# An attention layer's last border: earlier queries, query tiles kept in key buffers, and two output tiles started half

## The chip, the cores and the metric

The kernel runs on one core of a Trainium2 chip. The metric is the device time of one launch in microseconds, as the median of several runs; shorter is better. TensorE multiplies (PE in the profile, with its weight loads as PEld), VectorE (DVE), ScalarE (ACT) and GpSimd (POOL) work on tiles, and SyncE (SP) issues most of the transfers from memory.

## The reference, cut to what matters

Two layers of a diffusion backbone over 512 latent tokens and 256 context tokens, 1024 features wide. The change lies in layer 0, windowed attention with 16 query heads that share 4 key and value heads:

```
q, k, v = split(h @ w_qkv); q = rope(rms_norm(q)); k = rope(rms_norm(k))
for each block of 128 latent queries:
    scores = [q.k_context, q.k_window] / 8          (window: the block and its two neighbours)
    p = softmax([scores, sink]);  o = p[context].v_context + p[window].v_window
context queries: the same, over the 256 context keys alone
x = x + gate * (o_x @ w_o);  ctx = ctx + gate_c * (o_c @ w_o)
```

Then a SwiGLU layer, a retention layer and a second SwiGLU layer follow, which the change does not touch.

## The kernel before, in words

Features lie on the 128 partitions and tokens along the free axis, so a weight tile of 128 output features is a column of eight 128x128 blocks. To keep float32 accuracy on TensorE's faster format, each operand is split into a high and a low part (`split`, lines 162 to 165: ScalarE copies the high part, VectorE subtracts for the low one), and one product becomes three matmuls (`mm3`, lines 143 to 149).

Attention runs in four groups `g` of one key head and four query heads. Each group has six blocks `(s, b)`: four of latent queries (`s` = 0) and two of context queries (`s` = 1). I write a block as (g, i), where i is its place in the group's order. The loop is at lines 828 to 845, and `attend` does this for one block:

- `score` (line 678): per head, TensorE makes the scores in one of three PSUM banks `S`; VectorE evicts them with the mask and the running maximum (L704) into a row tile `pr`, of which there are nine; per pair of heads ScalarE takes exponentials (L101) and GpSimd divides by the sum (L717).
- `turn` (line 721): per key tile, TensorE transposes the four heads' probabilities (L726) into one of two PSUM banks `pT`, and ScalarE or VectorE, in turn, copies them out (L728).
- `output` (line 733): TensorE multiplies with the values (L740) into the one bank `pO`; VectorE copies the result to `o_raw` (L755), or, in the last group, splits it straight into `o_t`.

Between the blocks the loop places other work. `make_q(j)` (line 559) makes the query heads 2j and 2j+1: 24 matmuls 512 wide over the latent tokens, 24 matmuls 256 wide over the context tokens into the two PSUM banks `pj`, then `shape` (rope, split into `q` tiles) and `norms` (row factors; the scores use them at eviction). It is called after blocks 1 and 3 of groups 0 to 2, for the next group. `q` tiles come from a ring of nine: two per j for the latent tokens, one for the context. A group's key tiles `k` are two of a ring of eight, and are not read after the group's last latent block.

From block (2, 4) on, `PARTS_AT` says how many of the stored `o_raw` halves are split into `o_t` after each block (18 in all), so that the output projection has its operands. The stored tiles share a ring with the residual stream, so a split also frees the room into which `load_stream` loads the context and latent streams. In the last group (order: context block 0, latent 0, context 1, latent 1, 2, 3) `context_out(d, w)` makes context output tile d whole, 24 matmuls 256 wide over all eight feature blocks, for d = 2 after block 3, d = 3 and 0 after block 4, and d = 1 after block 5. Each needs its weights loaded (`w_raw`, a ring of two, on SP's queue) and split.

The loop as it stands:

```
    for g in range(NKV):
        final = g == NKV - 1
        for i, (s, b) in enumerate((latent + context, latent + context, mixed, late)[g]):
            copy = attend(g, s, b)
            if not final and i in (1, 3):
                for piece in make_q(2 * g + 2 + i // 3):
                    piece()
            if (g, i) >= SPLIT_AT:
                first = len(parts_o) == 18
                for _ in range(PARTS_AT[g, i]):
                    parts_o.pop(0)([copy])
                if first:
                    wo0 = wpos[0]
                    cres = load_stream(1)
            for d in {3: early[:1], 4: early[1:3], 5: early[3:]}.get(i, ()) if final else ():
                wpos[0] = wo0 + d
                wo_w[d] = next_w(ap, 0)
                context_out(d, wo_w[d])
```

After the loop the latent output projection follows, 24 matmuls 512 wide for each of eight tiles, a dense stretch for TensorE.

The order of instructions on each engine is settled by a scheduler at build time; every engine's queue then runs in that order, and an instruction that waits holds what is behind it.

Of the kernel before, what the change touches and what calls it, by code (L numbers as in the profile page):

```python
# [9 lines left out]
F32R = mybir.dt.float32r  # L10
# [4 lines left out]
P = 128  # L15
D = 1024
KT = D // P
SX = 512
SC = 256
HD = 64  # L20
NH = 16
NKV = 4
# [4 lines left out]
EPS = 1e-6  # L27
UNITS = (4, 5, 8, 6)
WO_ADA = [(0, d) for d in range(8)]
SPLIT_AT = (2, 4)  # L30
HALVES = (slice(0, 256), slice(256, 512))

C_ADAB = 0
# [16 lines left out]
def dit_kernel(ctx, tc, xT, cT, crow, small, consts, masks, tabs0, tabs1, jtab, adaQ, adaN, adaT, wst, out):  # L50
# [11 lines left out]
    def T(pool, cols, tag, bufs, dt=F32):  # L62
        return pool.tile([P, cols], dt, tag=tag, bufs=bufs, name=tag)

    def pj(n=512):
        return T(psJ, 512, "pj", 2)[:, :n]
# [51 lines left out]
    wpos, wsel, ring = [0], [0], []  # L118

    def w_raw(pool=None, bufs=2):  # L120
        raw = T(pool or rp, 1024, "wraw", bufs)
        nc.sync.dma_start(raw, wst[wpos[0]])
        wpos[0] += 1
        return raw

    def w_parts(pool, own=2):

        bufs = own
        if ring:
            pool, bufs = ring[wsel[0] % len(ring)], 2  # L130
        elif wsel[0] % (2 + own) < 2:
            pool, bufs = rp, 2
        wsel[0] += 1
        return T(pool, 1024, "whi", bufs, F32R), T(pool, 1024, "wlo", bufs, F32R)

    def next_w(pool, own=2, raw=None, behind=(), late=()):

        raw = raw or w_raw()
        w = w_parts(pool, own)
        after(split(raw, *w, behind), late)  # L140
        return w

    def mm3(o, w, x, first, last):

        whi, wlo = w
        xhi, xlo = x
        nc.tensor.matmul(o, whi, xhi, start=first, stop=False)  # L147
        nc.tensor.matmul(o, wlo, xhi, start=False, stop=False)  # L148
        return nc.tensor.matmul(o, whi, xlo, start=False, stop=last)  # L149

    def project(w, hs, o):
        for k in range(KT):
            mm3(o, (w[0][:, k * P:(k + 1) * P], w[1][:, k * P:(k + 1) * P]), hs[k], k == 0, k == KT - 1)
# [14 lines left out]
    def load_stream(s, engines=(nc.sync, nc.sync)):  # L168
        res = []
        if s == 0:  # L170
            for k in range(KT):
                t = T(rp, 512, "res", 12)
                eng = engines[k % 2] if k < 4 else nc.sync
                ins = eng.dma_start(t, xT[:, k, :])
                if eng is nc.scalar:
                    turn["lnexp"].append(ins)
                res.append(t)
        else:
            for k in range(0, KT, 2):
                t = T(rp, 512, "res", 12)  # L180
                nc.sync.dma_start(t.rearrange("p (a n) -> p a n", a=2), cT[:, k:k + 2, :])
                res += [t[:, 0:SC], t[:, SC:2 * SC]]
        return res

    def t_sq(n):
        return T(rp, 512, "sq", 2)[:, :n]
# [180 lines left out]
    akv = AK.enter_context(tc.tile_pool(name="akv", bufs=1, reuse_waits="tile"))  # L367
# [152 lines left out]
    ap = At.enter_context(tc.tile_pool(name="ap", bufs=1, reuse_waits="tile"))  # L520
# [36 lines left out]
    q, stats = {}, {}  # L557

    def make_q(j, raw=None):

        if raw is None:
            w = next_w(ap, 0)
            parts_of = lambda k: (w[0][:, k * P:(k + 1) * P], w[1][:, k * P:(k + 1) * P])
        else:

            rows = [[T(ap, 656, "pr", PRB, F32R)[:, :512] for _ in range(2)] for _ in range(2)]
            for i, (hi, lo) in enumerate(rows):
                split(raw[:, i * 512:(i + 1) * 512], hi, lo)  # L570
            parts_of = lambda k: [t[:, k % 4 * P:(k % 4 + 1) * P] for t in rows[k // 4]]
        qs = T(ap, 64, "qs", 4)[:, 0:36].rearrange("p (f n) -> p f n", f=3)
        sqs, o = [], [None, None]

        def part(s, k0, k1):
            if k0 == 0:
                o[s] = pj(NTOK[s])
            for k in range(k0, k1):
                mm3(o[s], parts_of(k), h[s][k], k == 0, k == KT - 1)

        def shape(s):
            n = NTOK[s]
            sq, qn = t_sq(n), t_hn(n)
            nc.scalar.activation(qn, o[s], AF.Identity, scale=qk_gain[:, 0:1])
            nc.scalar.activation(sq, o[s], AF.Square)
            sqs.append(sq)
            if s == 0:
                sw = t_y(s)
                nc.vector.stream_shuffle(sw, qn, swap16)
                nc.gpsimd.tensor_tensor(qn, qn, rope0[:, 0:512], op=mult)  # L590
                nc.vector.tensor_tensor(sw, sw, rope0[:, 512:1024], op=mult)
                nc.vector.tensor_tensor(qn, qn, sw, op=add)
            qa = T(ap, 512, "q", 9, F32R)
            if s == 0:
                qb = T(ap, 512, "q", 9, F32R)
            else:
                qa, qb = qa[:, 0:SC], qa[:, SC:2 * SC]
            nc.scalar.copy(qa[0:64, :], qn[0:64, :])
            nc.scalar.copy(qb[64:128, :], qn[64:128, :])
            nc.vector.tensor_tensor(qa[64:128, :], qn[0:64, :], qa[0:64, :], op=sub)  # L600
            nc.vector.tensor_tensor(qb[0:64, :], qn[64:128, :], qb[64:128, :], op=sub)
            q[2 * j, s] = qa
            q[2 * j + 1, s] = qb

        def norms():
            tot = pj(12)
            for s, sq in enumerate(sqs):
                for b in range(NTOK[s] // P):
                    c = 8 * s + 2 * b
                    nc.tensor.matmul(tot[:, c:c + 2], sq[:, b * P:(b + 1) * P], bd[:, 0:P:64], start=True, stop=True)  # L610
            y, u, z = qs[:, 0], qs[:, 1], qs[:, 2]
            neg_half_rstd(y, z, tot, HD)
            nc.vector.scalar_tensor_tensor(u, tot, HD * EPS, y, add, mult)
            ue = u.rearrange("p (b e) -> p e b", e=2)
            for e in range(2):
                hd = 2 * j + e
                nc.vector.tensor_scalar(ue[:, e], ue[:, e], nsink[:, hd:hd + 1], -4.0 / HD, op0=mult, op1=mult)
                stats[hd] = qs

        def first():  # L620
            part(0, 0, 5)

# [12 lines left out]
    with tc.manual_schedule(engines={mybir.EngineType.PE}):  # L635
# [10 lines left out]
        for e in range(2):  # L646
            k1, k2 = key_parts(e, kn[1], "kc", 4)
# [18 lines left out]
    o_t = [[None] * KT, [None] * KT]  # L666
# [143 lines left out]


    early = [2, 3, 0, 1]
    wo_w = {}

    def context_out(d, w):
        o = pj(SC)
        project(w, o_t[1], o)
        ins = gated_add(1, 0, 2, d, o, cres)
        add_square(1, int(d != early[0]), cres[d])
        return ins  # L820
# [1 line left out]
    latent, context = [(0, b) for b in range(4)], [(1, b) for b in range(2)]  # L822
    mixed = [latent[0], latent[1], context[0], latent[2], latent[3], context[1]]
    late = [context[0], latent[0], context[1], latent[1], latent[2], latent[3]]
    parts_o = [p for sb in ((0, 0, 0), (0, 1, 0), (1, 1, 0), (2, 1, 0), (0, 0, 1), (1, 0, 0), (1, 0, 1),
                            (2, 0, 0), (2, 0, 1)) for p in splits_o(*sb)]
    PARTS_AT = {(2, 4): 2, (2, 5): 3, (3, 0): 3, (3, 1): 2, (3, 2): 2, (3, 3): 2, (3, 4): 2, (3, 5): 2}
    for g in range(NKV):
        final = g == NKV - 1
        for i, (s, b) in enumerate((latent + context, latent + context, mixed, late)[g]):  # L830
            copy = attend(g, s, b)
            if not final and i in (1, 3):
                for piece in make_q(2 * g + 2 + i // 3):
                    piece()
            if (g, i) >= SPLIT_AT:
                first = len(parts_o) == 18
                for _ in range(PARTS_AT[g, i]):
                    parts_o.pop(0)([copy])
                if first:
                    wo0 = wpos[0]  # L840
                    cres = load_stream(1)
            for d in {3: early[:1], 4: early[1:3], 5: early[3:]}.get(i, ()) if final else ():
                wpos[0] = wo0 + d
                wo_w[d] = next_w(ap, 0)
                context_out(d, wo_w[d])
    assert not parts_o
    xr = load_stream(0)
# [10 lines left out]
    for d4 in range(0, KT, 4):  # L858
        wpos[0] = wo0 + max(d4, 2)
        w = [next_w(wo_p) if d > 1 else wo_w[d] for d in range(d4, d4 + 4)]  # L860
        if d4 == 0:
            cr = cond_rows(wo_p)
        for d in range(d4, d4 + 4):
            o = pj(SX)
# [304 lines left out]
    qa = R.enter_context(tc.tile_pool(name="qa", bufs=1, reuse_waits="tile"))  # L1169
# [168 lines left out]
    for hd in range(RH):  # L1338
# [172 lines left out]
        for i in range(2):  # L1511
            g, v = chunk(bg + i), chunk(bv + i)
# [70 lines left out]
        w = []  # L1583
# [335 lines left out]
```

## Time and profile before

| quantity | value |
|---|---|
| time, median of 3 runs (lowest to highest) | 1747.34 us (1747.12 to 1749.5) |
| span of the profiled execution, first to last instruction | 1744.4 us |
| its own time | not recorded apart; the median less the span is 2.9 us |
| TensorE / VectorE / ScalarE / GpSimd busy | 98% / 77% / 49% / 8% |
| norms of the last queries begin; value products of block (2, 4) end | 252.0 us; 270.1 us |

Times in the profile count from the first instruction. "Busy" of PE is modelled: matmuls are pipelined, so two neighbours overlap, and a PE that is busy may still be waiting in part. A column "PEclk" gives the granted clock, 1.00 being full speed. In rows of groups, the time behind "idle before" is what the engine waited before those instructions, with who ended the wait.

### The profile page before, as it was taken

To read this page: it belongs to the slowest core of one execution; us is meant where nothing else is said; L and a number is where in the kernel's file an instruction comes from. 1 tells how busy PE (TensorE), PEld (TensorE's weight loads), DVE (VectorE), ACT (ScalarE), POOL (GpSimd) and SP (SyncE) were. 2 spreads that over 40 slices of the span, in tenths; PEclk is the share of its full clock that TensorE was granted. 3 is DMA by queue.
4 is the path that set the end of the run, shared out by engine and by line. 5 is a ranking of instruction groups with operands and counts; after the bars stand their busy time and mean duration, and the time that the engine had idled before them with its cause. 6 is when DMAs were issued, how large, how long until landed. Compare 5 with 4: busy or idle time off the path is not lost.

```text
span 1744.4 us, 27605 instructions
## 1 busy us (share of the span) xinstructions
PE 1712.7 (98%) x10876; PEld 1527.8 (88%) x10876; DVE 1350.5 (77%) x2368; ACT 846.3 (49%) x1492; POOL 131.0 (8%) x270
## 2 busy tenths in 40 slices
PE   7999999999999999999999999999999999999999
PEld 5777777899999999999988888898898899999997
DVE  6697778788778788787889858758768798777774
ACT  5576667465433334342456534525525565445442
POOL 0035435000000000000000000000000000000000
PEclk9999999999999999999999999999999999999999
DMA  9501012533243534343423524423423224233322
GB/s 353 230 13 38 13 43 68 204 122 135 71 147 121 158 109 145 123 153 101 156 99 86 182 84 130 162 86 121 157 85 118 76 84 132 77 117 101 104 79 85
DMA packets 59602, 203.54 MB, mean 117 GB/s; under 512 B 6608, under 2 KB 6992, under 8 KB 59216
## 3 DMA queue, kind: packets, MB, share of 16 engines
q1 hardware_dynamic: 51984, 175.03, 30.9%
q0 software_dynamic: 7200, 26.22, 5.2%
q8 instruction: 85, 1.39, 0.3%
q10 hardware_dynamic: 288, 0.52, 0.1%
q14 instruction: 45, 0.37, 0.1%
HBM read 199.65 MB, written 2.10 MB: 116 GB/s over the span
## 4 chain that ended last, share of the span: by engine, by line
PE 80%; DVE 8%; DMA 5%; ACT 3%; issue 2%; POOL 1%; SPq 0%; ACTq 0%; POOLq 0%; DVEq 0%
PE Y L886 15%; PE Z L886 7%; PE pj L147 6%; PE pj L148 6%; PE pj L149 6%; PE Z L1268 6%; PE X L886 4%; PE Y L1257 3%; PE pj L1268 2%; PE pT L726 2%; PE X L1257 2%; DMA wraw<-in_wst_dram 2%; PE pO L740 2%; PE S L703 2%; DMA adan<-in_adaQ_dram 1%
## 5 line engine op out<-in xcount | busy, mean ns | idle before, releaser
L164 ACT CAST whi<-wraw 128x1024 fp32r<-128x1024 f32 x258 | 270.2, 1051 | 370.7 <-PE Z L149 88.5
L165 DVE TENSOR_TENSOR wlo<-wraw,whi 128x1024 fp32r<-128x1024 f32 x258 | 315.0, 1223 | 60.9 <-ACT whi L164 59.7
L886 PE MATMUL Y<-aq,whi 128*128 128x384 f32 x640 | 173.7, 335 | 0.5 <-ACT sq L1044 0.5
L256 DVE SCALAR_TENSOR_TENSOR res<-pj,mod,res 128x512 f32<-128x512 f32 (+1 forms) x112 | 81.5, 729 | 65.6 <-PE pj L149 65.0
L886 PEld LDWEIGHTS Y<-aq,whi 128*128 128x128 f32 x640 | 116.6, 188 | 1.7 <-ACT sq L1044 0.9
L273 DVE CUSTOM_DVE_ANT_0 y<-adaw,crow,small_sb 128x1024 bf16<-128x1024 f32 x64 | 81.9, 1280 | 36.0 <-DMA adaw<-in_adaT_dram 35.7
L886 PE MATMUL Y<-aq,wlo 128*128 128x384 f32 x320 | 107.0, 334 | 0.0
L101 ACT ACTIVATE pr<-pr,stat,qs 128x513 f32<-128x513 f32 (+2 forms) x96 | 74.4, 777 | 23.5 <-DVE stat L710 22.9
L1268 PE MATMUL Z<-whi,sA 128*128 128x512 f32 x256 | 81.0, 391 | 1.2 <-ACT gate L1454 1.2
L717 POOL TENSOR_SCALAR pr<-pr,stat 128x512 f32<-128x512 f32 (+2 forms) x96 | 70.2, 744 | 79.5 <-DVE stat L714 54.8
L147 PE MATMUL pj<-ax,whi 128*128 128x512 f32 x176 | 68.8, 391 | 0.1
L149 PE MATMUL pj<-ax,whi 128*128 128x512 f32 x176 | 68.7, 390 | 0.0
L148 PE MATMUL pj<-ax,wlo 128*128 128x512 f32 x176 | 68.5, 389 | 0.0
L147 PE MATMUL pj<-act,whi 128*128 128x512 f32 x168 | 66.0, 393 | 0.0
L148 PE MATMUL pj<-act,wlo 128*128 128x512 f32 x168 | 65.9, 392 | 0.0
L149 PE MATMUL pj<-act,whi 128*128 128x512 f32 x168 | 65.5, 390 | 0.0
L270 POOL DMA_DIRECT2D adaw<-in_adaT_dram x48 | 25.6, 533 | 514.9 <-DVE mod L273 413.6
L726 PE MATMUL pT<-const_sb,pr 128*128 128x128 f32 x352 | 57.4, 285 | 6.1 <-POOL pr L717 3.6
L886 PE MATMUL Y<-sA,whi 128*128 128x256 f32 x304 | 60.6, 282 | 0.2 <-ACT res L1721 0.2
L886 PEld LDWEIGHTS Y<-aq,wlo 128*128 128x128 f32 x320 | 60.1, 188 | 0.0
L726 PEld LDWEIGHTS pT<-const_sb,pr 128*128 128x128 f32 x352 | 39.1, 142 | 23.0 <-POOL pr L717 12.4
L1268 PEld LDWEIGHTS Z<-whi,sA 128*128 128x128 f32 x256 | 48.0, 188 | 11.7 <-ACT gate L1454 1.9
(576 smaller groups left out, 5150.3 us busy)
## 6 DMA issues: line engine op xcount, KB each, us to landing
wraw<-in_wst_dram SPq DMA_DIRECT2D x224, 512.0 KB, 3.7
adaw<-in_adaT_dram POOLq DMA_DIRECT2D x48, 512.0 KB, 3.9
wx<-in_wst_dram SPq DMA_DIRECT2D x30, 512.0 KB, 4.3
adan<-in_adaQ_dram SPq DMA_DIRECT2D x16, 512.0 KB, 8.5
adan<-in_adaN_dram SPq DMA_DIRECT2D x12, 512.0 KB, 7.8
adaw<-in_adaT_dram SPq DMA_DIRECT2D x8, 512.0 KB, 3.9
res<-in_xT_dram SPq DMA_DIRECT2D x14, 256.0 KB, 3.8
aq<-in_adaN_dram SPq DMA_DIRECT2D x12, 256.0 KB, 5.8
```

Source lines behind the costliest of these rows:

```text
L101: ins = nc.scalar.activation(*args, **kw)
L147: nc.tensor.matmul(o, whi, xhi, start=first, stop=False)
L148: nc.tensor.matmul(o, wlo, xhi, start=False, stop=False)
L149: return nc.tensor.matmul(o, whi, xlo, start=False, stop=last)
L164: after(nc.scalar.copy(hi, t), behind)
L165: return nc.vector.tensor_tensor(lo, t, hi, op=sub)
L256: return nc.vector.scalar_tensor_tensor(res[d], o, mods[l, s][:, part, d:d + 1], res[d], mult, add)
L273: res.append(nc.vector.tensor_tensor_reduce(junk, w, cr[:, s * 1024:(s + 1) * 1024], 1.0, sm_t[:, C_ADAB + l * 48 + j:C_ADAB + l * 48 + j ...
L726: nc.tensor.transpose(tp[:, a * P:(a + 1) * P], self.pr[(0, 2, 1, 3)[a]][:, ki * P:(ki + 1) * P], ident)
L886: nc.tensor.matmul(o, p, r, start=first and k + i == 0, stop=k == 3 and i == 2, skip_group_check=not first)
L1257: ins = nc.tensor.matmul(o[:, e * SC:(e + 1) * SC], p[:, ws], r, start=first and k + e + i == 0, stop=k == 3 and i == 2, skip_group_check= ...
L1268: ins = nc.tensor.matmul(os[t], p, r, start=first and k + i == 0, stop=k == 3 and i == 2, skip_group_check=by_k or not first)
```

## The change

- `make_q` for the last group's queries (j = 6 and 7) is called after blocks 0 and 2 of group 2, where it was called after 1 and 3. Groups 0 and 1 keep 1 and 3.
- For j = 5 and 7 the two latent query tiles come from the ring of key tiles `k` (room of groups 0 and 1, which are done), not from the ring `q`.
- The splits of stored outputs start after block (2, 3), two after each block, and in another order: the context halves of groups 0 and 1 come first.
- New: `context_begin(d, behind)` loads and splits the weights of context tile d and makes its first half, the 12 matmuls over feature blocks 0 to 3 (heads 0 to 7), into a `pj` bank that stays held. It is called for d = 2 after block (2, 4) and for d = 3 after block (2, 5). `context_out` then makes the other 12 where it made all 24. Both `pj` banks are held from there until those tiles are done.

```
-SPLIT_AT = (2, 4)
+SPLIT_AT = (2, 3)
...
-            qa = T(ap, 512, "q", 9, F32R)
+            room = (akv, 512, "k", 8, F32R) if s == 0 and j in (5, 7) else (ap, 512, "q", 9, F32R)
+            qa = T(*room)
             if s == 0:
-                qb = T(ap, 512, "q", 9, F32R)
+                qb = T(*room)
...
+    def context_part(o, w, k0, k1):
+        for k in range(k0, k1):
+            mm3(o, (w[0][:, k * P:(k + 1) * P], w[1][:, k * P:(k + 1) * P]), o_t[1][k], k == 0, k == KT - 1)
+
+    def context_begin(d, behind):
+        wpos[0] = wo0 + d
+        wo_w[d] = next_w(ap, 0, behind=behind)
+        begun[d] = pj(SC)
+        context_part(begun[d], wo_w[d], 0, 4)
+
     def context_out(d, w):
-        o = pj(SC)
-        project(w, o_t[1], o)
+        o = begun.pop(d, None)
+        if o is None:
+            o = pj(SC)
+            project(w, o_t[1], o)
+        else:
+            context_part(o, w, 4, KT)
...
-    parts_o = [p for sb in ((0, 0, 0), (0, 1, 0), (1, 1, 0), (2, 1, 0), (0, 0, 1), (1, 0, 0), (1, 0, 1),
+    parts_o = [p for sb in ((0, 1, 0), (1, 1, 0), (0, 0, 0), (2, 1, 0), (0, 0, 1), (1, 0, 0), (1, 0, 1),
                             (2, 0, 0), (2, 0, 1)) for p in splits_o(*sb)]
-    PARTS_AT = {(2, 4): 2, (2, 5): 3, (3, 0): 3, (3, 1): 2, (3, 2): 2, (3, 3): 2, (3, 4): 2, (3, 5): 2}
+    PARTS_AT = {(2, 3): 2, (2, 4): 2, (2, 5): 2, (3, 0): 2, (3, 1): 2, (3, 2): 2, (3, 3): 2, (3, 4): 2, (3, 5): 2}
+    BEGIN_AT = {(NKV - 2, 4): early[0], (NKV - 2, 5): early[1]}
...
-            if not final and i in (1, 3):
-                for piece in make_q(2 * g + 2 + i // 3):
+            if not final and i in ((0, 2) if g == NKV - 2 else (1, 3)):
+                for piece in make_q(2 * g + 2 + i // 2):
...
+            if (g, i) in BEGIN_AT:
+                context_begin(BEGIN_AT[g, i], [copy])
             for d in {3: early[:1], 4: early[1:3], 5: early[3:]}.get(i, ()) if final else ():
-                wpos[0] = wo0 + d
-                wo_w[d] = next_w(ap, 0)
+                if d not in wo_w:
+                    wpos[0] = wo0 + d
+                    wo_w[d] = next_w(ap, 0)
                 context_out(d, wo_w[d])
```

More of the change, by code (lines that the diff above doesn't have):

```diff
@@ L812, in dit_kernel @@
     early = [2, 3, 0, 1]
-    wo_w = {}
-    def context_out(d, w):
-        o = pj(SC)
-        project(w, o_t[1], o)
+    wo_w, begun = {}, {}
+    def context_part(o, w, k0, k1):
[6 more added lines that the diff above has]
+        context_part(begun[d], wo_w[d], 0, 4)
+    def context_out(d, w):
+        o = begun.pop(d, None)
[4 more added lines that the diff above has]
+            context_part(o, w, 4, KT)
         ins = gated_add(1, 0, 2, d, o, cres)
```

## The prediction

> **What bounds the kernel now.** I read the page first, then the stretches of the attention layer, then who waits for whom in the slowest of them.
>
> ```profile
> span 1744.4 us, 27605 instructions
> PE 1712.7 (98%) x10876; PEld 1527.8 (88%) x10876; DVE 1350.5 (77%) x2368; ACT 846.3 (49%) x1492; POOL 131.0 (8%) x270
> ...
> PE 80%; DVE 8%; DMA 5%; ACT 3%; issue 2%; POOL 1%; SPq 0%; ACTq 0%; POOLq 0%; DVEq 0%
> ```
>
> TensorE is the bound: it carries 80% of the chain that ended last. The change removes no matmul, so it can only remove TensorE's waiting. The built program's order shows that the queues differ only from block (1, 4) to the last block of attention; from there TensorE's order is the same again. So the whole effect lies within about 205 to 318 us:
>
> ```profile
> core 0: us, PE busy (x) PEld busy (x) DVE busy (x) ACT busy (x) POOL busy (x), PEclk, DMA share, GB/s
> 205.20:252.00 46.80, 45.70 (x312) 35.65 (x309) 34.90 (x120) 30.48 (x74) 22.41 (x46) 1.00 0.12 40
> 252.00:270.10 18.10, 15.69 (x109) 12.21 (x107) 14.79 (x51) 13.67 (x35) 5.55 (x16) 0.91 0.10 30
> 270.10:318.20 48.10, 46.44 (x358) 37.37 (x356) 39.04 (x127) 34.52 (x89) 20.34 (x43) 1.00 0.22 67
> ...
> 258.00:262.00 4.00, 2.43 (x13) 1.57 (x11) 3.97 (x22) 3.07 (x7) 0.70 (x2) 0.93 0.00 0
> 262.00:264.00 2.00, 2.00 (x9) 1.82 (x9) 1.45 (x8) 1.44 (x6) 2.00 (x3) 0.50 0.04 8
> ```
>
> The middle row is the border: 109 matmuls in 18.1 us, where the row above has 312 in 46.8. VectorE is full in 258 to 262 (3.97 of 4.00) while TensorE is busy 2.43 of 4.00, and right after that the granted clock is 0.50. Busy overstates TensorE's work, as matmuls overlap, so I price the work by the step from one group of matmuls to the next:
>
> ```profile
> 252.00 1.40 PE L610 MATMUL pj<-const_sb,sq 128*128 128x2 f32 x12
> 253.26 0.49 PE L703 MATMUL S<-kc,q 128*128 128x256 f32 x2
> ...
> 254.26 0.40 PE L703 MATMUL S<-kc,q 128*128 128x256 f32 x2
> 254.50 0.41 PE L703 MATMUL S<-k,q 128*128 128x256 f32 x2
> ...
> 237.97 0.51 PE L703 MATMUL S<-k,q 128*128 128x384 f32 x2
> 238.31 0.39 PE L147 MATMUL pj<-h,whi 128*128 128x512 f32 x1
> 238.55 0.39 PE L703 MATMUL S<-kc,q 128*128 128x256 f32 x2
> ...
> 314.54 1.09 PE L726 MATMUL pT<-const_sb,pr 128*128 128x128 f32 x8
> 315.39 0.37 PE L148 MATMUL pj<-hc,wlo 128*128 128x256 f32 x1
> ...
> 308.04 2.38 PE L740 MATMUL pO<-tt,v 128*64 128x256 f32 x20
> 310.35 0.33 PE L726 MATMUL pT<-const_sb,pr 128*128 128x128 f32 x1
> ```
>
> So a norm product costs 0.105 us, a 256-wide matmul 0.12, a 384-wide one 0.17, a 512-wide one 0.24, a transpose 0.107, a value product 0.117.
>
> **The border now.** Its products, counted up to the end of block (2, 4)'s values:
>
> ```profile
> L703 PE MATMUL S<-kc,q 128*128 128x256 f32 x25 | 6.7, 360 | 1.6 <-DVE qs L200 1.0 <-DVE stat L704 0.4
> L726 PE MATMUL pT<-const_sb,pr 128*128 128x128 f32 x26 | 4.6, 311 | 0.8 <-ACT tt L728 0.5 <-POOL pr L687 0.3
> L740 PE MATMUL pO<-tt,v 128*64 128x256 f32 x36 | 4.3, 385 | 0.0
> L703 PE MATMUL S<-k,q 128*128 128x256 f32 x10 | 2.3, 298 | 0.0
> ```
>
> 35 x 0.12 + 24 x 0.107 (two of the 26 are older) + 36 x 0.117 + 12 x 0.105 = 12.2 us of work in 18.1: 5.9 lost. Counted the same way over the queue's order, 205.2 to 252.0 holds 41.4 us of work in 46.8 (ratio 1.13) and 270.1 to 318.2 holds 42.3 in 48.1 (1.14). At that ratio the border would take 13.8; it costs 4.3 us more, and this is what there is to win. In the border no projection stands between scores and transposes, so TensorE waits for VectorE's evictions, then for exponentials, normalisations and copies.
>
> **Part by part.** *Query tiles in key buffers.* Today the last queries' casts stand late, since their room in the ring of nine was that of queries which block (2, 4) still read:
>
> ```profile
> 254.47 0.75 DVE L704 CUSTOM_DVE_ANT_0 pr<-S,mask,qs 128x512 f32<-128x512 f32 x1 [1.57 <-PE S L703]
> 255.02 0.62 ACT L598 CAST q<-hn 64x512 fp32r<-64x512 f32 x1
> ```
>
> It comes after block (2, 4)'s first score eviction. The key tiles that take their place were last read in groups 0 and 1, so no wait is added, and casts and scores keep their shapes: cost 0, gain only through the order.
>
> *Queries a block sooner.* In the built order the 48 matmuls of the last queries (24 x 0.24 + 24 x 0.12 = 8.6 us) end 36 matmuls earlier, before block (2, 3)'s scores and not after them. They are a filler, and what they leave is longer. From their norms to the first product of context tile 2 the new order has 43 scores of 256, 8 of 384, 40 transposes, 44 value products, 12 norm products: 5.1 + 1.4 + 4.3 + 5.1 + 1.3 = 17.2 us, 5.0 more than today's 12.2. Before them stands 5.0 us less, at ratio 1.13 worth 5.65: the norms begin at 252.0 - 5.65 = 246.35.
>
> How long the 17.2 takes I follow along the queues, with these rows:
>
> ```profile
> L704 DVE CUSTOM_DVE_ANT_0 pr<-S,mask,qs 128x256 f32<-128x256 f32 x40 | 18.4, 478 | 3.7 <-PE S L703 2.7 <-PE pT L726 0.8
> L728 DVE COPY tt<-pT 128x512 f32<-128x512 f32 x24 | 16.5, 689 | 7.3 <-PE pT L726 7.0
> L704 DVE CUSTOM_DVE_ANT_0 pr<-S,mask,qs 128x512 f32<-128x512 f32 x16 | 11.7, 742 | 1.7 <-PE S L703 1.6
> L704 DVE CUSTOM_DVE_ANT_0 pr<-S,mask,stat 128x384 f32<-128x384 f32 x16 | 9.7, 609 | 0.1
> ...
> L717 POOL TENSOR_SCALAR pr<-pr,stat 128x640 f32<-128x640 f32 x16 | 15.1, 954 | 10.0 <-DVE stat L714 8.1 <-ACT h L164 1.8
> ...
> L590 POOL TENSOR_TENSOR hn<-hn,rope 128x512 f32<-128x512 f32 x2 | 3.0, 1491 | 0.6 <-DVE y L589 0.6
> ```
>
> Each VectorE instruction starts some 0.07 us before the one ahead ends, so I take 0.40, 0.54 and 0.67 for evictions of 256, 384, 512, and 0.61 for a copy. Counted from the norms: VectorE starts on block (2, 3)'s scores at about 1.7, as the rope product on GpSimd (1.49) and the casts and copies behind it come first. From there to the reciprocal of that block's second pair it has 4 x 0.40 + 4 x 0.54 + 4 x 0.67 (block (2, 4) is evicted in between) and 2.6 of query parts, a value copy and small ones: 9.0, to 10.7. Two normalisations, 1.9: 12.6. Four more turns through the two transpose banks, each 0.43 and a copy, partly side by side: 3.4, to 16.0. From there TensorE has 20 + 16 value products, 16 transposes and 11 scores in a row: 7.0, to 23.0. Hand-overs that I left out, 0.6 by the waits on `tt` and `pr` in the border's rows: 23.6. So the border ends at 246.35 + 23.6 = 269.95, against 270.1 at the same amount of work: -0.15. The gap moves a block forward more than it shuts. Bounds: 17.2 x 1.13 = 19.4 (all waits as in the neighbours) and 17.2 x 18.1/12.2 = 25.5 (today's efficiency).
>
> *Two half tiles.* 24 matmuls, 24 x 0.12 = 2.9 us, move ahead from the last group; they bring no work and stand behind the gap, since they need the weights' low part, which VectorE makes at the end of that run (1.2 us each, now after block (2, 4)'s copy; today one of them came before the border). What they hide is the start of the last group. The split of a low part, VectorE's load from 270.1 to 300.0, and TensorE's own waits from 270.1 to 318.2 today:
>
> ```profile
> L165 DVE TENSOR_TENSOR wlo<-wraw,whi 128x1024 fp32r<-128x1024 f32 x3 | 3.6, 1212 | 0.0
> 270.10:300.00 29.90, 28.79 (x221) 23.91 (x221) 26.92 (x97) 23.00 (x61) 15.05 (x37) 1.00 0.18 54
> PE pT L726 <- POOL pr L717: 1.4, 4, 0.5
> ```
>
> With 2.9 us of matmuls in hand VectorE gets ahead, and I take -1.0 of these 1.4. Bounds: -1.4, and +2.9 if the places that lose this filler stand idle instead. `pj`: both banks stay held, and nothing else asks for one in that time.
>
> *Splits and loads.* 18 splits as before, only in another order: 0 on TensorE's path. On SP's queue the weights of tiles 0 and 1 now stand behind all context loads and the first latent ones:
>
> ```profile
> 245.72 1.37 SPq L181 DMA_DIRECT2D res<-in_cT_dram  x3
> 265.20 0.33 SPq L122 DMA_DIRECT2D wraw<-in_wst_dram  x1
> 269.36 0.33 SPq L181 DMA_DIRECT2D res<-in_cT_dram  x1
> 270.03 21.71 SPq L174 DMA_DIRECT2D res<-in_xT_dram  x5
> ...
> wraw<-in_wst_dram SPq DMA_DIRECT2D x5, 512.0 KB, 3.5
> ```
>
> A split in block (3, 1), near 285, releases the second latent load and with it tile 1's weights; they land 3.5 us after issue, and ScalarE wants them only after block (3, 2). There it now has both casts in a row, the second waiting until tile 3 has left its weight buffer; the copies and exponentials of blocks (3, 3) and (3, 4) are queued behind. By the order TensorE is done with tile 3 before the first cast ends, so 0; if not, TensorE waits as long. The later layers keep their order: 0.
>
> Sum: -0.15 - 1.0 = -1.15. The span of the profiled execution, the only time recorded of it, becomes 1743.2; the median of the runs lies 1747.34 - 1744.4 = 2.9 above the span, so the time is **1746.2 us**. Its own bounds, from -2.5 to +2: 1744.8 to 1749.3.
>
> **The clock.** After a thin stretch (2.43 busy of 4.00) the clock was 0.50 for 3.4 us. The new order has a thin stretch too, between 7 and 14 us after the norms, where scores and 22 transposes fill about half of the time; none between 262 and 268 today was thinner, and the clock came back there. I take no drop. The Trainium skill, "TensorE: Matmul & The Clock Gate", Part 1, says that the gate halves the clock after a window of about 3.4 us found idle, that the window runs freely, and, in Part 4, that transposes do not count as busy. The halving and its length agree with the trace; the thin stretch here was not wholly idle, so the trace is stricter than the page; that transposes count for nothing speaks against the change, whose gap is filled by them.
>
> **Rivals.**
> 1. *The gap shuts.* If VectorE evicts block (2, 3) while the earlier projection still runs, the border takes 19.4, not 23.6: 4.2 us less, 1742.0. For it: VectorE is busy only 35.65 of 46.80 ahead of the border, so it has time; against it: the order puts those scores behind the norms.
> 2. *The gap grows.* With no filler for 17.2 us of work the border runs at today's efficiency, 25.5, and the places in the last group that lose 2.9 us of filler stand idle: +1.9 and +3.9 on the forecast, 1752.0. It decides once VectorE, 27 of 30 us busy after the border, can't catch up. For it: 3.97 of 4.00 in 258 to 262.
> 3. *The clock falls again.* 3.4 us at half clock lose 1.7 us of work: 1747.9.
> That nothing changes because the half tiles stand behind the gap is the forecast's own middle (1747.3).
>
> **How the numbers follow.** Forecast 0.36, rival 1 0.33, rival 2 0.20, rival 3 0.11. A measurement of this kernel can tell about 0.2%, 3.5 us, from no change: 1743.8 and 1750.8. Rival 1 is faster by more, rival 2 slower, the other two within, with 0.03 for their edges: faster 0.35, same 0.44, slower 0.21. The range reaches into both: 1741.0 to 1751.2, with most of rival 1 and the milder half of rival 2. The forecast's own is 1744.8 to 1749.3.
>
> **What would show it.** In the profile after: norms of the last queries near 246; the first product of tile 2 near 270; VectorE full in the stretch between, TensorE's waits there for `pr`, `tt` and `stat`; whether the clock stays at 1.00; the last value products of attention near 317. A border under 20 us, or one over 25, would prove me wrong, as would a wait of ScalarE for weights in the last group.

## The result: 1751.1 us, 0.24% slower

The changed kernel takes 1751.12 us (median of 19 runs, 1749.0 to 1752.82); the kernel before, in runs on the same chips, 1747.34 us (19 runs, 1744.81 to 1749.5). The ratio is 1.0024, 95% interval 1.0018 to 1.003: 3 to 5 us slower. The forecast was 1746.2 us.

The head of the page after, with the shares of the chain that ended last:

```profile
span 1749.3 us, 27598 instructions
PE 1714.9 (98%) x10876; PEld 1526.8 (87%) x10876; DVE 1351.4 (77%) x2368; ACT 846.4 (48%) x1492; POOL 130.6 (7%) x270
...
PE 84%; DVE 6%; DMA 3%; ACT 3%; issue 2%; POOL 1%; SPq 0%; ACTq 0%; DVEq 0%; POOLq 0%
```

The same number of working instructions on every engine, and a span 4.9 us longer. Not all of that is the change. In every run since, the time is 1.7 to 1.8 us above the span, so the profiled execution before, with its span of 1744.4, took about 1746.2 us, less than the median. And the first norm product after block (1, 2), ahead of anything that was moved, starts at 202.20 here and at 200.56 in the profile before:

```profile
200.56 0.95 PE L610 MATMUL pj<-const_sb,sq 128*128 128x2 f32 x8
```

```profile
202.20 0.95 PE L611 MATMUL pj<-const_sb,sq 128*128 128x2 f32 x8
...
247.91 0.95 PE L611 MATMUL pj<-const_sb,sq 128*128 128x2 f32 x8
...
272.65 0.38 PE L147 MATMUL pj<-hc,whi 128*128 128x256 f32 x1
```

This start differs by up to 1.7 us between executions, so 1.64 must come off every time of this profile before it is set beside the other (lines below attention's head stand one lower after the change: L704 is L703 of before, and so on). Then the last queries' norms begin at 246.27 (252.0 before) and the border ends, with the first product of context tile 2, at 271.01. The three stretches after, from the windows view (busy us and count of each engine, granted clock):

```profile
206.86:247.91 41.05, 39.63 (x272) 31.30 (x269) 27.43 (x96) 25.05 (x63) 18.11 (x41) 1.00 0.10 33
247.91:272.72 24.81, 21.99 (x150) 15.44 (x148) 20.88 (x72) 19.02 (x47) 9.42 (x23) 1.00 0.06 18
272.72:324.25 51.53, 48.09 (x358) 37.76 (x357) 40.63 (x129) 34.64 (x88) 20.50 (x43) 1.00 0.24 76
```

and the last one before, cut at the same two points, the ends of the value products of block (2, 4) and of the last block:

```profile
270.18:318.46 48.28, 46.62 (x357) 37.38 (x357) 39.14 (x127) 34.45 (x89) 20.34 (x43) 1.00 0.22 67
```

The border is now 24.81 us (24.74 to the first product of tile 2) with TensorE busy in 21.99, and its clock stays at 1.00. The stretch behind it holds the same work as before, the half tiles included, and takes 51.53 us for 48.28.

**How the runs are compared.** I call *excess* of a kernel at a block: the time from the end of block (1, 1)'s value products to the end of this block's, less the same time before, less the difference in TensorE work that the built orders put ahead of those two points (matmuls at the prediction's prices). It is the waiting that was added up to there, whatever was moved. Each value is from one profiled execution; five kernels with one order in the border and no clock fall there agree within 0.06 us.

| kernel | ratio, 95% interval | (2,4) | (3,0) | (3,3) | (3,5) |
|---|---|---|---|---|---|
| the whole change | 1.0024, 1.0018 to 1.0030 | +0.9 | +2.5 | +3.3 | +4.1 |
| e1 queries sooner | 1.0021, 1.0012 to 1.0030 | +3.4 | +3.4 | +3.4 | +3.4 |
| e2 half tiles and splits | 1.0039, 1.0026 to 1.0053 | +3.8 | +5.4 | +6.2 | +7.1 |
| e3 splits' order | 1.0017, 1.0008 to 1.0026 | +0.3 | +0.4 | +4.0 | +4.1 |
| e4 room in key buffers | 1.0003, 0.9994 to 1.0012 | +0.6 | +0.6 | +0.7 | +0.6 |
| e5 no half tiles | 1.0011, 1.0002 to 1.0020 | +3.2 | +3.2 | +2.5 | +2.5 |
| e6 one half tile | 1.0025, 1.0014 to 1.0036 | +0.9 | +2.6 | +4.7 | +4.8 |
| e7 half tiles in the border | 1.0018, 1.0009 to 1.0027 | +0.9 | +0.8 | +3.6 | +3.4 |
| e8 idle products, after | 1.0035, 1.0023 to 1.0048 | -0.5 | +1.1 | +1.9 | +2.8 |
| e9 fifth tile, after | 1.0032, 1.0020 to 1.0043 | +1.2 | +2.8 | +4.0 | +3.6 |
| e10 fifth tile, before | 1.0019, 1.0010 to 1.0028 | 0.0 | 0.0 | 0.0 | +1.2 |
| e11 fifth tile, no half tiles | 1.0029, 1.0019 to 1.0039 | +4.0 | +4.0 | +4.4 | +4.0 |
| e12 idle products, before | 1.0006, 0.9997 to 1.0015 | -1.0 | -1.0 | -1.0 | -1.0 |
| e13 no half tiles, splits held | 1.0018, 1.0009 to 1.0026 | +0.9 | +1.1 | +3.4 | +3.4 |
| e14 half tiles later | 1.0019, 1.0010 to 1.0028 | +0.9 | +1.9 | +3.6 | +3.6 |
| e15 later still | 1.0007, 0.9998 to 1.0016 | +0.9 | +1.8 | +1.7 | +1.5 |
| e16 queries sooner, splits held | 1.0033, 1.0021 to 1.0046 | +0.6 | +1.8 | +5.4 | +6.1 |
| e17 queries as before, half tile in border | 1.0006, 0.9997 to 1.0015 | -0.6 | -0.4 | +2.5 | +2.3 |
| e18 half tiles latest | 1.0022, 1.0013 to 1.0031 | +1.8 | +2.7 | +3.6 | +4.1 |

Ratios are to the kernel before on the same chip. They are not quotients of the medians given below; where the two differ (e2, 1.0044 by the medians; e17, 1.0013) the ratio with its interval counts. e8 and e12 carry 2.8 and 1.9 us of products more, whose cost is in the ratio and not in the excess. So the whole change loses 0.9 us in the border and 3.2 behind it.

### The profile page after: what moved, and what is told of

The parts are those of the page before. It is cut to its first block, busy times and chain, and to the rows that moved or that the text cites. A ratio compares the mean times of both kernels' runs of the same rounds, so it can differ in the third digit from the quotient of the medians.

```text
span 1749.3 us, 27598 instructions
## 1 busy us (share of the span) xinstructions
PE 1714.9 (98%) x10876; PEld 1526.8 (87%) x10876; DVE 1351.4 (77%) x2368; ACT 846.4 (48%) x1492; POOL 130.6 (7%) x270
## 4 chain that ended last, share of the span: by engine, by line
PE 84%; DVE 6%; DMA 3%; ACT 3%; issue 2%; POOL 1%; SPq 0%; ACTq 0%; DVEq 0%; POOLq 0%
PE Y L905 15%; PE Z L905 7%; PE Z L1287 7%; PE pj L147 6%; PE pj L148 6%; PE pj L149 6%; PE X L905 4%; PE Y L1276 3%; PE pj L1287 2%; PE pT L727 2%; PE X L1276 2%; PE X L149 1%; PE X L147 1%; PE X L148 1%; PE pO L741 1%
```

## The experiments

**The parts alone.** e1 takes the moved calls of `make_q` and the rooms, e3 `SPLIT_AT`, the new order of `parts_o` and `PARTS_AT` (with them the context loads come a block sooner), e4 the rooms; e2 is the change with `i in (1, 3)` and the old ring put back.

```
e1:  i in ((0, 2) if g == NKV - 2 else (1, 3))   and   room = (akv, 512, "k", 8, F32R) ...
e3:  SPLIT_AT = (2, 3);  parts_o: (0, 1, 0), (1, 1, 0), (0, 0, 0), ...;  PARTS_AT = two after each block
e4:  room = (akv, 512, "k", 8, F32R) if s == 0 and j in (5, 7) else (ap, 512, "q", 9, F32R)
```

> The last group's queries a block sooner, with their tiles in freed key buffers; splits and context tiles as before. Theory A (the last group loses its filler to the half tiles): only the longer unfilled border is left, +0.9 us by the trace of the whole change, so 1748.2, and the last group runs as before. Theory B (the long border itself puts VectorE late, and the last group pays): nearly all of the loss is here, 1751. Theory C (the new order of the splits is what costs): 1747.5 to 1748.

> The two half tiles, with the new order of splits that they need; queries where they were before, in their own ring. Theory A: the loss of the last group is here, +2.5 to +3.2 us, 1750 to 1750.5. Theory B: nothing to lose without the long border, 1747.3, or 1746 if the half tiles hide what they were said to hide. Theory C: about +2, 1749.5, as in the run with the splits alone.

> Only the new order and places of the splits of stored outputs, and with them the context loads a block sooner. Theories A and B: no change, 1747.3 within 0.7. Theory C: slower by 2 us or more, 1749.5.

> Only the query tiles of j = 5 and 7 in key buffers; their calls stay. All theories: the casts of the last queries no longer follow block (2, 4), which costs nothing by itself; between -0.6 us (the stall of 1.2 at the border's start goes in part) and 0: 1746.7 to 1747.3.

Measured, against 1748.43 before: 1751.97, 1756.11, 1751.6 and 1748.78. None of the theories fits all of them: queries 3.5, splits 3.2 and half tiles with splits 7.7, where the whole is 3.8. The parts don't add up, so each moves something that the others move too. Only the room behaves: nothing that can be measured. The excess says where each loses: e1 in the border, e2 there and behind it, e3 by the end of block (3, 3). In e3 this is mainly one wait and the clock behind it; the timelines of VectorE, GpSimd and TensorE, and the windows ahead of and behind the fall:

```profile
299.75 0.16 DVE L714 RECIPROCAL stat<-stat 128x2 f32<-128x2 f32 x1
299.88 1.22 DVE L165 TENSOR_TENSOR wlo<-wraw,whi 128x1024 fp32r<-128x1024 f32 x1
301.01 0.75 DVE L704 CUSTOM_DVE_ANT_0 pr<-S,mask,qs 128x512 f32<-128x512 f32 x1
...
299.86 1.28 POOL L687 COPY pr<-qs 128x1 f32<-128x1 f32 x1 [3.12 <-PE pT L726]
...
302.19 0.33 PE L726 MATMUL pT<-const_sb,pr 128*128 128x128 f32 x1 [1.47 <-POOL pr L717]
...
299.41:302.82 3.41, 1.94 (x14) 1.41 (x15) 3.41 (x9) 3.41 (x7) 2.96 (x5) 1.00 0.24 34
302.83:306.24 3.41, 3.41 (x20) 1.75 (x16) 1.26 (x4) 0.68 (x3) 0.50 (x1) 0.50 0.59 202
```

VectorE and ScalarE are full for the whole 3.41 us, and a weight split of 1.22 us stands among VectorE's evictions; TensorE waits 1.47 us for normalised probabilities, and right behind this thin window the clock is 0.50 for 3.41 us. The split isn't ahead of that chain in VectorE's queue: the reciprocal that GpSimd needs (299.75) comes before it. What it holds up is GpSimd. The one-column copy that GpSimd makes ahead of the normalisation takes 1.28 us, to the end of the split; the same copy in the kernel before, with no split beside it:

```profile
297.59 0.18 POOL L687 COPY pr<-qs 128x1 f32<-128x1 f32 x1 [3.01 <-PE pT L726]
```

This is not special to e3. Over all twenty profiles, GpSimd's normalisation of 640 columns took 0.79 to 0.82 us in the 314 cases in which VectorE ran at most evictions and other work out of PSUM or small factors at the same time; in the 86 cases in which a weight split ran beside it for 0.1 us or more, the median was 1.69 us. It doesn't cost TensorE time each time: in the kernel before, a normalisation took 2.05 us at 298.75, and TensorE did not wait behind it.

**With and without half tiles, and filler.** e5 drops `context_begin` from the change; e6 keeps tile 2's only; e7 begins the two tiles after (2, 2) and (2, 3) and splits the context halves of groups 0 and 1 there; e8 adds products that nobody reads.

```
e6:  BEGIN_AT = {(NKV - 2, 4): early[0]}
e7:  BEGIN_AT = {(2, 2): early[0], (2, 3): early[1]};  SPLIT_AT = (2, 2);  PARTS_AT: 4 at (2, 2), 2 at (2, 3), ...
e8:  for k in range(8): mm3(o2, parts_of(k), h[1][k], k == 0, k == 7)     # after the last norms
```

> The whole change without the two half tiles (queries sooner, their tiles in key buffers, the new order of splits; all four context tiles whole in the last group). Theory A (the half tiles take the last group's filler): the last group's loss of 3.2 us goes, the border stays: 1 to 2 us over the kernel before. Theory D (the three parts cost 3 us each and only happen to cancel in the whole): queries 3.5 and splits 3.2 add up, 6 to 7 us over the kernel before. Theory E (the half tiles' work helps the border, the split order hurts the last group): 5 us over.

> The whole change with only tile 2 begun early; tile 3 whole in the last group. Theory A: half of the last group's loss, so between the whole change and the one without half tiles, about 2.5 us over the kernel before. Theory D: no rule between them, 3 to 6 over.

> The whole change, with the halves of tiles 2 and 3 begun two blocks sooner: after blocks (2, 2) and (2, 3), and the context halves of groups 0 and 1 split before them. By the built order tile 2's half then stands right behind the last norms and tile 3's among the transposes of the border. If the border is bound by VectorE and by hand-overs, their 2.8 us of TensorE work fit into its waits: the border keeps its 24.7 us and 2.8 us less stands behind it, so about 1 us over the kernel before. If TensorE's own work counts there, nothing is won: 3.8 over, as the whole change. The last group stays without this filler in both.

> The whole change with 24 further products of 256 right behind the last norms, ahead of block (2, 3)'s later scores; they repeat products of the query projection on the context tokens, and their result is not read. That is 2.8 us of TensorE work. If VectorE, not TensorE, sets the border's time: 0 to +0.8 us over the whole change. If TensorE's own work counts: +2.8. If they also keep the clock from falling in executions where it falls: up to 1.7 us under the whole change.

Measured, against 1748.5: 1750.37, 1752.22, 1751.15 and 1753.65. Without half tiles (e5) the last group loses nothing more (from +3.2 at its start to +2.5), as theory A says, but the border loses 3.2 in place of 0.9, which no theory had. With one (e6) the loss behind the border is larger than with two (3.9 for 3.2), against theory A's half. In e7 the border took 2.8 us more of wanted work at the same excess, and the last group lost 2.7 again by block (3, 3). In e8, 1.4 of 2.8 us of added work vanished in the border's waits: half of its time is TensorE's own there, half is not.

Why e5's border is longer is seen in its timelines (VectorE, GpSimd, TensorE) and windows:

```profile
258.39 1.20 DVE L165 TENSOR_TENSOR wlo<-wraw,whi 128x1024 fp32r<-128x1024 f32 x1
259.90 0.17 DVE L715 RECIPROCAL stat<-stat 128x2 f32<-128x2 f32 x1 [0.31 <-ACT pr L101]
...
258.57 1.69 POOL L718 TENSOR_SCALAR pr<-pr,stat 128x640 f32<-128x640 f32 x1 [1.54 <-DVE stat L715]
...
260.24 0.80 POOL L718 TENSOR_SCALAR pr<-pr,stat 128x640 f32<-128x640 f32 x1
...
260.31 1.22 PE L727 MATMUL pT<-const_sb,pr 128*128 128x128 f32 x6 [1.64 <-POOL pr L718]
...
258.00:262.00 4.00, 1.77 (x10) 0.98 (x9) 2.06 (x7) 3.21 (x10) 3.43 (x4) 1.00 0.35 78
262.20:265.70 3.50, 3.50 (x17) 2.97 (x18) 1.90 (x9) 1.97 (x5) 2.17 (x7) 0.51 0.70 267
```

Here tile 2's weights are split inside the border, since nothing holds that split back; in the whole change `behind=[copy]` holds it until block (2, 4) is copied. GpSimd's normalisation beside it takes 1.69 us, the next one 0.80, and TensorE waits 1.64 us for the first. TensorE is busy 1.77 of 4.00, and the clock falls just as the transposes and value products come that were waited for.

**More real filler.** A fifth context tile, 7, is made in the last group and not in the dense stretch behind.

```
early = [2, 3, 7, 0, 1]
e9, e11:  {3: early[:2], 4: early[2:4], 5: early[4:]}      e10:  {3: early[:1], 4: early[1:4], 5: early[4:]}
```

> The whole change, and context tile 7 made whole in the last group beside tiles 2, 3, 0 and 1 (early = 2, 3, 7, 0, 1; two of them released after block 3, two after block 4, one after block 5), and not in the dense stretch behind. Its weights are loaded and split once more. Theory A (the last group lacks filler): of its 2.8 us of TensorE work some 2 fit into waits, and the dense stretch is 2.8 shorter: 1.5 to 2.5 us under the whole change. Rival (VectorE and ScalarE set the last group's time, not the lack of filler): the second split adds 1.2 us on VectorE and 1.0 on ScalarE there, 0 to 1 us over the whole change.

> The kernel before with the same fifth tile (one released after block 3, three after block 4, one after block 5). Theory A: the last group before still waits about 4 us behind block (3, 3), so 0.5 to 1.5 us under the kernel before. Rival: 0 to 1 over.

> The change without half tiles, with the fifth tile. Theory A: 0.5 to 1.5 us under the one without half tiles, so about 1 us over the kernel before. Rival: 2 to 3 over.

Measured, against 1747.1: 1752.46, 1750.44 and 1751.8: slower by about 3 us in the kernel before, against theory A. Most of this arises behind attention. At the end of its last block e10 has lost 1.2 us; behind it, in the dense stretch that now lacks the tile, TensorE waits once for ScalarE's first operands of the SwiGLU layer, in e9 and e11 as long as in e10 and not in the kernel before:

```profile
378.17 0.44 PE L147 MATMUL X<-aq,whi 128*128 128x384 f32 x1 [1.89 <-ACT aq L920]
```

In e10 the clock falls once more behind that wait. So these runs don't refute that filler was missing in the last group: behind the border e9 loses 2.4, less than the change's 3.2, while e11 does not gain on e5. The built order could put the tile's products only behind block (3, 2), most of them in lumps near the end, and its weight split is one more on VectorE. They do refute that more of it helps wherever it lands.

**Idle products in the border of before.** Four behind each head's first eviction in block (2, 4):

```
ins = nc.tensor.matmul(extra, kx[g][0][:, 0:P], kx[g][0][:, 0:SC], ...); after(ins, [evs[g, s, b][-1]])
```

> The kernel before with 16 further products of 256 among the scores of block (2, 4), four behind each head's first eviction; they multiply a key tile with itself and their result is not read: 1.9 us of TensorE work into the stretch where TensorE waits most. If the border's time is VectorE's and the work keeps the clock from falling there (1.7 us): 0.5 to 1.5 us under the kernel before. If VectorE sets the time and the clock falls all the same: 0 to +0.5. If TensorE's own work counts: +1.9.

Measured 1748.56 against 1747.1 (ratio 1.0006, 0.9997 to 1.0015). Its windows:

```profile
252.44:271.60 19.16, 17.08 (x126) 12.91 (x125) 15.31 (x51) 13.91 (x36) 5.79 (x16) 1.00 0.20 69
258.00:262.00 4.00, 3.29 (x26) 2.96 (x24) 3.88 (x15) 2.51 (x6) 0.00 (x0) 1.00 0.87 309
```

VectorE is as full as before (3.88 of 4.00, 3.97 there), TensorE busy 3.29, not 2.43, and the clock did not fall. The stretch from the norms to the border's end is 19.16, not 18.1, with 1.9 us more in it: half is hidden, and the rest costs. The built order also moved the border's weight split, from 263.93 to 255.58, so that the clock held because of the products alone is not shown.

**Splits held, half tiles later.** e13 and e16 hold the weight splits of tiles 2 and 3 behind the copies of (2, 4) and (2, 5); e14, e15 and e18 begin the half tiles later in the whole change.

```
e13, e16:  wo_w[d] = next_w(ap, 0, behind=[copies[HOLD[d]]] if d in HOLD else ());  HOLD = {2: (2, 4), 3: (2, 5)}
e14:  BEGIN_AT = {(2, 5): early[0], (3, 0): early[1]}
e15:  BEGIN_AT = {(3, 0): early[0], (3, 1): early[1]}
e18:  BEGIN_AT = {(3, 1): early[0], (3, 2): early[1]}
```

> The change without half tiles, but the weight splits of tiles 2 and 3 wait for the copies of blocks (2, 4) and (2, 5), as they do in the whole change. By the built order the border is then instruction for instruction the one of the whole change. If the split ahead of the reciprocal and the clock's fall behind it made the border longer: the border's excess falls from 3.2 to 0.9 us and the time to 0 to 1 us over the kernel before. If the half tiles themselves shortened it: 3 at the border, 2 to 2.5 over.

> The whole change with the two half tiles begun later: tile 2 after block (2, 5), tile 3 after block (3, 0). Their 24 products then stand between the scores of the first blocks of the last group instead of in a lump ahead of them. Border as in the whole change, 0.9. If the lump is what costs (VectorE idle behind it, then scores at VectorE's pace): the 1.6 us lost by the end of block (3, 0) go, and the whole is about 2 us over the kernel before. If filler that is missing later costs: the loss moves to blocks (3, 2) to (3, 4), about 4 over, as the whole change.

> The same, with tile 2 begun after block (3, 0) and tile 3 after block (3, 1). If the lump costs: 1 to 2 us over the kernel before. If missing filler costs, less of it is missing behind, and the loss shrinks with the place: 2 to 3 over.

> The queries a block sooner alone, splits in the old order, with the weight splits of tiles 2 and 3 held as in the run before. If the split in the border was the cause of its 3.3 us: 0.9 there, and 0 to 1.5 us over the kernel before in all, with an uncertain part behind block (3, 2), where the built order now puts more of the tiles' products late. If not: 3.5 over, as without the hold.

> The whole change with tile 2's half begun after block (3, 1) and tile 3's after block (3, 2), one block later than in the run that came to 1.5 us over by its trace. If only the place ahead of the last group's first blocks costs: 0.5 to 1.5 us over the kernel before. If filler is now missing in blocks (3, 0) and (3, 1): 2 to 3 over, with the loss there.

Measured: 1749.88, 1749.09, 1747.82 and 1752.6 against 1746.42, and 1750.98 against 1746.78. e13 settles the border: with the split held, and no half tile anywhere, its excess is 0.9 as in the whole change, not 3.2. Its windows from the norms to the end, and where e5 was thin:

```profile
246.68:271.48 24.80, 21.96 (x150) 15.41 (x149) 21.09 (x77) 19.02 (x48) 9.45 (x23) 1.00 0.06 17
258.00:262.00 4.00, 3.15 (x18) 2.07 (x18) 2.06 (x9) 3.94 (x10) 3.00 (x5) 1.00 0.00 0
```

But the time did not follow (3.5 over, expected 0 to 1): the held split of tile 3 then stands at 283.0, where GpSimd's normalisation beside it takes 1.66 us for 0.69, and TensorE waits 0.98 for it:

```profile
283.00 1.25 DVE L165 TENSOR_TENSOR wlo<-wraw,whi 128x1024 fp32r<-128x1024 f32 x1
...
282.48 0.69 POOL L718 TENSOR_SCALAR pr<-pr,stat 128x512 f32<-128x512 f32 x1 [2.06 <-DVE stat L711]
283.15 1.66 POOL L718 TENSOR_SCALAR pr<-pr,stat 128x512 f32<-128x512 f32 x1
...
284.86 0.44 PE L727 MATMUL pT<-const_sb,pr 128*128 128x128 f32 x2 [0.98 <-POOL pr L718]
```

That wait is 1.0 of the 2.5 us that e13 loses behind its border; the rest was not taken apart. e16 is the same with the old splits: 0.6 in the border, where e1 had 3.4 with a split at 259.67 in it, and 5.5 behind it. Beginning the half tiles later shrinks the last group's loss from 3.2 (change) to 2.7 (e14) and 0.6 (e15), and one block later it is 2.3 again (e18). e15 is the best form of the change that was run, and not told apart from the kernel before; its stretch behind the border takes 49.10 us for the 51.53 of the change:

```profile
247.28:272.08 24.80, 21.98 (x150) 15.43 (x149) 20.84 (x75) 18.08 (x47) 9.42 (x23) 1.00 0.06 17
272.08:321.18 49.10, 47.22 (x359) 37.67 (x358) 40.36 (x127) 35.72 (x88) 21.20 (x43) 1.00 0.25 80
```

e18 also shows the price of a fall by itself, since its border has the order of e13, e14 and e15. They end it at +0.9, e18 at +1.8, with the clock at half from 260.86:

```profile
257.00:261.00 4.00, 2.86 (x16) 1.81 (x16) 2.64 (x9) 3.95 (x10) 3.03 (x5) 0.98 0.00 0
260.90:264.30 3.40, 3.40 (x17) 2.87 (x16) 2.05 (x8) 1.99 (x6) 1.91 (x6) 0.50 0.00 0
```

**The kernel before with half a tile in its border.** Queries stay; tile 2's first half stands behind the evictions of block (2, 4), three products a head, and the context halves of groups 0 and 1 are split after (2, 1) and (2, 2).

```
context_part(begun[2], wo_w[2], i, i + 1, [evs[g, s, b][-1]])      # in block (2, 4), after head i
```

> The kernel before with queries at their old places and old ring, and with the first half of tile 2 in the border: three products behind each head's first eviction in block (2, 4). The context halves of groups 0 and 1 are split after blocks (2, 1) and (2, 2), so that they and the weights of tile 2 are ready. By the run with idle filler there (16 products, excess of the border 1.0 us lower): 12 products, 1.4 us of wanted work, into waits, so the border's excess falls by about 1; the last group loses that filler. If the split order's loss in block (3, 3) (3.0 us in the run with the splits alone) comes back here: 1.5 to 3 us over the kernel before. If not: 0.5 under to 0.5 over.

Measured 1749.0 against 1746.78 (ratio 1.0006, 0.9997 to 1.0015). The border did take the work (excess -0.6, with 2.8 us of tiles 2 and 3 in it by the built order), and by block (3, 3) 3.1 were lost again. No version that was run beats the kernel before.

## Why the prediction was wrong

The forecast was -1.15 us; the trace has +0.9 in the border and +3.2 behind it. That 1751.1 still lies just inside the wide range to 1751.2 says nothing for it: that end was held open for rival 2, and the forecast's own bounds end at 1749.3.

- *Query tiles in key buffers, cost 0*: held (e4, ratio 0.9994 to 1.0012).
- *Norms at 246.35*: held, 246.27.
- *The border, 23.6 from the norms, -0.15 in all*: 24.74 and +0.9. Its steps, in the timelines of VectorE, GpSimd and TensorE, counted from 247.91:

```profile
259.22 0.15 DVE L715 RECIPROCAL stat<-stat 128x2 f32<-128x2 f32 x1
...
259.47 2.91 POOL L718 TENSOR_SCALAR pr<-pr,stat 128x640 f32<-128x640 f32 x4 [0.85 <-DVE stat L715]
...
265.06 2.38 PE L741 MATMUL pO<-tt,v 128*64 128x256 f32 x20
```

  The reciprocal of block (2, 3)'s second pair comes at 11.3 (10.7 forecast), that pair is normalised at about 13.1 (two of GpSimd's four, 0.80 us each for the 0.95 of the forecast, whose row mixed in ones with a weight split beside them; 12.6), the long run with the value products begins at 17.15 (16.0) and takes 7.6 (7.0, which is 7.2 by the forecast's own prices, and 0.6 for hand-overs). VectorE's part was short by 0.6, and the turns through the transpose banks by another 0.6, 4.0 for 3.4. The size was off, the mechanism not: the gap moved forward and didn't shut, so rival 1 is out.
- *Half tiles, -1.0*: this failed. The stretch behind the border, which was to gain 1.0, lost 3.2, though not all by the half tiles. The forecast saw them put VectorE ahead. In the timelines of the change (VectorE and ScalarE) the opposite is seen:

```profile
270.88 1.21 DVE L165 TENSOR_TENSOR wlo<-wraw,whi 128x1024 fp32r<-128x1024 f32 x1
...
273.44 1.22 DVE L165 TENSOR_TENSOR wlo<-wraw,whi 128x1024 fp32r<-128x1024 f32 x1
274.58 0.16 DVE L715 RECIPROCAL stat<-stat 128x2 f32<-128x2 f32 x1
...
277.46 0.61 ACT L101 ACTIVATE pr<-pr,stat,qs 128x257 f32<-128x257 f32 x1 [3.57 <-DVE stat L711]
...
278.21 0.75 DVE L705 CUSTOM_DVE_ANT_0 pr<-S,mask,qs 128x512 f32<-128x512 f32 x1 [0.87 <-PE S L704]
```

  While TensorE makes the half tiles, VectorE spends 2.4 us on two weight splits, ScalarE waits 3.57 for factors, and then VectorE itself waits 0.87 for scores that stand behind the half tiles. By the end of block (3, 0) this is 1.6 of the 3.2; with later half tiles (e14, e15, e18) it is 0.9 to 1.0 there, with none (e13) 0.2. The other 1.6 is spread over blocks (3, 1) to (3, 5), where the half tiles' filler is gone. The longest wait in it, in block (3, 4), again follows a stretched normalisation (VectorE, GpSimd, TensorE):

```profile
308.66 1.21 DVE L165 TENSOR_TENSOR wlo<-wraw,whi 128x1024 fp32r<-128x1024 f32 x1
...
308.70 1.83 POOL L718 TENSOR_SCALAR pr<-pr,stat 128x640 f32<-128x640 f32 x1
...
310.59 0.44 PE L727 MATMUL pT<-const_sb,pr 128*128 128x128 f32 x2 [1.15 <-POOL pr L718]
```

  The half tiles are not the whole cause: e13 has none and loses 2.5 behind its border, e15 has both and loses 0.6.
- *Splits and loads, 0*: this failed too. e3 moves nothing else and costs 3.2 us. The forecast had 18 splits as before and so nothing on TensorE's path; it had no term for what a weight split does to GpSimd. The order decides which GpSimd instruction a 1.2 us weight split runs beside, this one is stretched by 0.9 to 1.1 us, and TensorE then waits 1.47 (e3), 1.64 (e5) or 0.98 us (e13). Two pairs of runs took the split out of the border, and the wait went with it: e5 against e13 (excess 3.2 and 0.9), e1 against e16 (3.4 and 0.6). That GpSimd's standstill is the link is read from the traces; no run gave its work to another engine. ScalarE's wait for weights, which the prediction named as a sign, did not come.
- *The clock, no drop*: held in the profile of the change (1.00 throughout the border), but not in the borders of e1, e2, e5, e9, e11 and e18. The thin stretch that was named is real, and that the clock held there was partly luck: e9 and e18 have the same order of work up to their falls.
- *Rivals.* Number 2, the gap grows, gave 1752.0 by a border of 25.5 and 2.9 us of idle places in the last group. Measured 24.74 and 3.2: its first half happened only in part, and the second agrees in size, but its reason isn't shown, as e13 keeps that filler and loses 2.5 there. Number 3 priced a fall at 1.7; e18 shows 0.9, and e9, whose clock fell at 254.5 where TensorE waited for VectorE anyway, only 0.3.

What stays open: no run took single splits out of the last group one by one, so how its loss divides between the weight splits' places, the half tiles' own place and the missing filler is argued from the timelines, not shown.

## What to carry to other kernels

Filler that TensorE does while it would wait may be a stock: what is brought forward to one gap is missing in the next. Here no move of wanted work won more than 0.6 us at the border (e17), and each form with half tiles lost 0.6 to 3.9 behind it. When a change only reorders, equal counts per engine say little; follow each long instruction on the engine next to the bound (here the 1.2 us split on VectorE) to the place where the order now has it, and ask which instruction it holds up that TensorE waits for, on other engines too (here GpSimd's copy or normalisation). Parts of such a change don't add: 3.5, 3.2 and 7.7 us for parts of a whole of 3.8.

## What the runs showed of the hardware

GpSimd stands still while VectorE splits a weight tile from SBUF: a one-column copy took 1.28 us beside the split and 0.18 without (e3, before), a normalisation of 640 columns 1.69 and 0.80 (e5). Beside evictions and other work out of PSUM it keeps its 0.79 to 0.82 us (314 cases).

The clock falls to 0.50 for 3.41 us behind a thin window, not only an idle one. In the attention layer of all profiles, the 3.41 us ahead of a fall had TensorE busy 0.93 (e2) to 2.51 us (e9); counted in steps of 3.41 us from each profile's own fall, 19 of the 28 windows with 2.0 to 2.5 us had no fall behind them. e2, busy 0.93, and e11, busy 1.74, stayed at half for 6.83 us; in e2:

```profile
259.06:262.47 3.41, 0.93 (x6) 0.70 (x6) 3.35 (x9) 1.19 (x3) 0.00 (x0) 1.00 0.00 0
262.47:269.30 6.83, 6.51 (x24) 4.90 (x22) 4.42 (x24) 5.18 (x15) 3.59 (x6) 0.50 0.01 2
```

The Trainium skill, "TensorE: Matmul & The Clock Gate", Part 1, says that the window of 3413 ns runs freely and that a kernel's behaviour varies with its phase. The runs agree: with one order of the border the clock fell in e18 and not in e13, e14 and e15. Part 1 also has the clock halved after an idle window; in these traces windows with up to 2.51 us of TensorE work did it, and the measurement decides.
